# Channel sums of x² taken on TensorE block by block, and the additions of x left to VectorE alone, at the ends of the layers of a two-layer encoder

## The chip, the cores and the metric

The kernel runs on one core of one Trainium2 chip. The metric is the device time of one execution in microseconds (us). Engines are named as the profile names them: PE is TensorE's matmul, PEld its weight load, DVE is VectorE, ACT is ScalarE, POOL is GpSimd, SP is SyncE, which starts the weight transfers.

## The reference

Two layers of a streaming encoder over 256 prompt frames and 64 sample frames (320 tokens, width 1024). Layer 0 is a Mamba-2 mixer, layer 1 an attention with a shared latent; each is followed by a convolutional feed-forward. Every sub-layer is wrapped in norms:

```
def rmsnorm(x, g):
    xf = x.astype(F32)
    y = xf * lax.rsqrt(jnp.mean(xf * xf, axis=-1, keepdims=True) + EPS)
    return (y * g.astype(F32)).astype(x.dtype)
...
for layer in range(DEPTH):
    h = rmsnorm(x, norm_mix_pre[layer])
    mix = ...                                   # mixer of this layer
    x = x + rmsnorm(mix, norm_mix_post[layer])
    f, fbuf = conv_ffn(rmsnorm(x, norm_ffn_pre[layer]), ...)
    x = x + rmsnorm(f, norm_ffn_post[layer])
```

So at the end of a sub-layer y is normalized and added to x, and the next sub-layer needs the mean of the new x² over the 1024 channels of each token.

## The kernel before, in words

**Layout.** Channels lie on the 128 partitions. `x` is a tile of 8 blocks of 128 channels by 320 tokens, and so are `y` (the sub-layer's output) and `xgh`, `xgl`. Matmuls run at float32 quality in three passes (`mm3`): each operand is split into a rounded high part and the low rest (`xgh`/`xgl` for x, `wh`/`wl` or, for units split ahead of time, `eh`/`el` for weights), and high·high, high·low and low·high are summed. A weight unit is fetched by SP into `wr`, split by ACT (high, L327 or L330) and DVE (low, L329 or L331), and taken from a stream by `nextw`.

**The ends.** There are four places where a sub-layer begins with fresh x, all in `enter`. At the start of the program (`boundary=False`) x is loaded. The other three are ends of sub-layers: mixer to feed-forward in layer 0 (near 266 us), feed-forward to attention (near 510 us), attention to feed-forward in layer 1 (near 733 us). There `late_rstd` makes the scale 1/rms of y for each token on POOL (L340) and spreads it over the partitions by three transposes on PE (L359) into one PSUM tile; between these PE runs bfloat16 filler matmuls (L365). Then, for block k = 0..7, `enter` does

- DVE: y(k) times the scale, which is read from that PSUM tile (L442);
- x(k) plus y(k) (L446), on DVE for k = 0, 1, 2, 4, 6 and on POOL for k = 3, 5, 7;
- ACT: the high part xgh(k) (L411; block 0's is made by DVE, L444);
- DVE: the low part xgl(k-1) (L418, or L421 without a gain), and behind xgl(1) and xgl(2) the low part of a weight unit;
- ACT: the square of x(k-1) (L433, block 0's by L430), and POOL adds it to `xacc` (L434).

In this region DVE and ACT keep the written order (`manual_schedule`); all other order is chosen by the scheduler when the program is built. Every engine executes its own list strictly in order.

**What follows.** PE runs the first matmuls of the next sub-layer (`outer`): for each x block k, six output blocks of 128 columns, 18 matmuls of 320 columns (block 0 at L583, the others at L284 and L285; 12 matmuls at the program's start; at the attention nine at a time for blocks 4 to 7). Their output is scaled afterwards, so they don't wait for the mean of x². That comes from `toksum`: three float32 matmuls with `xacc` as weights and a column of ones (L352), which the profile shows as six weight loads and six matmuls; DVE turns the sums into a mean (L346), POOL into 1/rms (L340), PE spreads it.

**PSUM.** Eight banks are divided into pools: `pm` for outputs, `px` for scratch and `pr` for sums and spread scales. The attention has no `pr` (its pools are 5 `pm` and 3 `px`), so at its end the spread scale lies in a `px` tile; `ffn` closes these pools behind `enter` and opens 7 `pm` and 1 `pr`.

**Weights ahead.** `early_open` fetches and splits some units of the next sub-layer during the last matmuls of the mixer or the feed-forward; `EARLY` says how many at each of the three ends.

Of the kernel before, what the change touches and what calls it, by code (L numbers as in the profile page):

```python
# [11 lines left out]
AF = mybir.ActivationFunctionType  # L12
ALU = mybir.AluOpType
# [3 lines left out]
P = 128  # L17
T = 320
TP = 256
TS = 64  # L20
D = 1024
KD = 8
NBF = 22
EPS = 1e-6
# [15 lines left out]
AHEAD = 1, 2  # L40

RING = 2, 3, 2
EARLY = 1, 9, 3
HIGH = 2, 0, 2
PSA = dict(m=5, x=3)
PSF = dict(m=7, r=1)
# [8 lines left out]
TOK = 0, 128, 192  # L55
# [31 lines left out]
class Kern:  # L87
# [252 lines left out]
        self.nw_end = self.nc.gpsimd.tensor_tensor(out=r, in0=v, in1=self.half[:, 0:v.shape[1]], op=ALU.pow).ins  # L340
        return r

    def mean(self, src, dim, pool):

        v = self.t(pool, [P, 3], "nwv", bufs=3)
        self.nc.vector.tensor_scalar(v, src, 1.0 / dim, EPS, op0=ALU.mult, op1=ALU.add)  # L346
        return v

# [5 lines left out]

    def spread(self, r, ps=None):

        ps = self.pr() if ps is None else ps
        for c, l0 in enumerate(TOK):
            self.pe_end = self.nc.tensor.transpose(ps[:, l0:l0 + 128], r[:, c:c + 1].to_broadcast([P, P]), self.ident).ins  # L359
        return ps[:, :T]  # L360
# [35 lines left out]
            self.high_ahead(HIGH[b])  # L396
        return ps

    def enter(self, xgp, sp, tag, g=None, boundary=True):


        nc = self.nc
        tt, act = nc.vector.tensor_tensor, nc.scalar.activation
        r = self.late_rstd() if boundary else None
        xh = self.t(xgp, [P, KD, T], "xgh", F32R, bufs=1)
        xl = self.t(xgp, [P, KD, T], "xgl", F32R, bufs=1)
        acc = self.t(sp, [P, T], "xacc", bufs=1)
        self.xhigh = []

        def high(k):  # L410
            i = act(out=xh[:, k, :], in_=self.x[:, k, :], func=AF.Copy, scale=self.v(g, k) if g and k else 1.0)  # L411
            if boundary:
                self.xhigh.append(i.ins)

        def low(k):
            h = xh[:, k, :].bitcast(F32)
            if g and k:
                i = nc.vector.scalar_tensor_tensor(out=xl[:, k, :], in0=self.x[:, k, :], scalar=self.v(g, k), in1=h,  # L418
                                                   op0=ALU.mult, op1=ALU.subtract)
            else:  # L420
                i = tt(out=xl[:, k, :], in0=self.x[:, k, :], in1=h, op=ALU.subtract)  # L421
            self.low_end = i.ins
            if boundary and k in AHEAD:
                self.gate = i.ins
                if self.lows:
                    self.lows.pop(0)()

        def square(k):
            if k == 0:
                act(out=acc, in_=self.x[:, k, :], func=AF.Square)  # L430
                return
            s = self.t(sp, [P, T], tag, bufs=2)
            act(out=s, in_=self.x[:, k, :], func=AF.Square)  # L433
            nc.gpsimd.tensor_tensor(out=acc, in0=acc, in1=s, op=ALU.add)  # L434

        with self.region if boundary else ExitStack():
            for k in range(KD + 1):
                if k < KD:
                    xk = self.x[:, k, :]
                    if boundary:  # L440
                        yk = self.y[:, k, :]
                        tt(out=yk, in0=yk, in1=r, op=ALU.mult)  # L442
                        if k == 0:
                            tt(out=xh[:, k, :], in0=xk, in1=yk, op=ALU.add)  # L444
                        e = nc.gpsimd if k in (3, 5, 7) else nc.vector
                        e.tensor_tensor(out=xk, in0=xk, in1=yk, op=ALU.add)  # L446
                        if k:
                            high(k)
                        else:
                            low(k)  # L450
                    else:
                        high(k)
                        low(k)
                if boundary and k > 1:
                    low(k - 1)
                if k:
                    square(k - 1)
        if boundary:
            self.ends.pop(0)
        return xh, xl, acc  # L460

    def normalized(self, xgp, sp, g, rstd):

# [123 lines left out]
            s = slice(b * 128, b * 128 + 128)  # L587
            self.mm3(ps[b][:, :T], w[k][0][:, s], w[k][1][:, s], xh[:, k, :], xl[:, k, :], k == 0, k == KD - 1, behind)

    def outer(self, nblk, xh, xl, xacc, pool):  # L590

        ps = [self.pm() for _ in range(nblk)]
        a, b = OUT
        self.outer_part(ps, range(a), xh, xl)
        r = self.rstd_of(xacc, D, pool)
        self.gate = self.nw_end
        self.outer_part(ps, range(a, b), xh, xl, self.pe_end)
        r = self.rstd_sb(r, pool, "xr")
        self.outer_part(ps, range(b, KD), xh, xl, self.pe_end)
        self.xhigh = []  # L600
        return ps, r
# [96 lines left out]
    def ssm(self):  # L698
        nc, a = self.nc, self.a
        self.silus, self.exps, self.burst = [], [], []  # L700
        self.yg, self.dc, self.ea = {}, {}, {}
        with ExitStack() as st:
# [5 lines left out]
            with ExitStack() as s2:  # L708
                sx = ExitStack()
                xgp = self.pool(sx, "xn0", "right")  # L710
                sp = self.pool(s2, "ssm")
                self.ssave = self.t(sp, [P, 24, 2, 3], "ssave")
                with ExitStack() as s3:
# [7 lines left out]
                    nc.sync.dma_start(out=self.con, in_=a["con"][:, 0:CON["cos"][0]])  # L721
                    nc.sync.dma_start(out=self.vec[:, 8:], in_=a["vec"][:, 8:])
                    self.qd = KD
                    xh, xl, xacc = self.enter(xtp, dp, "xsq", "mix_pre0", False)
                    ps, rstd = self.outer(4, xh, xl, xacc, dp)
                    self.bt, self.ct, self.xs = {}, {}, {}
                    dt2 = self.ssm_dt(ps[0], rstd, sp, dp)
                    for i in range(1, 4):
# [306 lines left out]
    def ffn(self, i):  # L1035
        nc, a = self.nc, self.a
        with ExitStack() as st:
# [3 lines left out]
            with ExitStack() as s2:  # L1041
                xgp = self.pool(s2, f"xgf{i}")
                sp = self.pool(s2, f"fs{i}")
                fsave = self.t(sp, [P, 44, 2, 2], "fsave")
                xh, xl, xacc = self.enter(xgp, sp, "xsq", f"ffn_pre{i}")
                self.yst.close()
                self.psum(**(PSF, PSL)[i])
                ps, rstd = self.outer(6, xh, xl, xacc, sp)
                self.est.close()
                self.table(AF.Gelu_apprx_tanh)  # L1050
                xnh, xnl, steps = self.normalized(xgp, sp, f"ffn_pre{i}", rstd)
# [39 lines left out]
    def mla(self):  # L1091
        nc, a = self.nc, self.a
        tt, ts, stt = nc.vector.tensor_tensor, nc.vector.tensor_scalar, nc.vector.scalar_tensor_tensor
        with ExitStack() as st:
# [10 lines left out]
            with ExitStack() as s2:  # L1105
# [3 lines left out]
                oldt = self.t(sp, [P, 2, 256], "oldt")  # L1109
                nc.sync.dma_start(out=old, in_=a["old"].rearrange("p (a b) -> p a b", a=3))  # L1110
                nc.sync.dma_start(out=oldt, in_=a["oldt"].rearrange("p (a b) -> p a b", a=2))
                xh, xl, xacc = self.enter(xgp, sp, "xsq")
                self.yst.close()
                self.psum(**PSF)
                u = self.t(kp, [P, 2, T], "u")
# [5 lines left out]
                kv, ps = pk[:3], pk[3:]  # L1121
                self.outer_part(pk, range(4), xh, xl)
                self.outer_part(kv, range(4, 8), xh, xl)
                s = self.t(sp, [P, T], "xsq", bufs=2)
                nc.scalar.activation(out=kacc, in_=kv[0][:, :T], func=AF.Square)
                nc.scalar.activation(out=s, in_=kv[1][:, :T], func=AF.Square)
                tt(out=kacc, in0=kacc, in1=s, op=ALU.add)
# [6 lines left out]


                pt = self.pr()
                self.toksum(xacc, pt)
                self.toksum(kacc, pt, 3)
                vs = self.t(sp, [P, 6], "vs")
                ex = self.t(sp, [P, 3], "ex")  # L1140
                ts(vs[:, 0:3], pt[:, 0:3], 1.0 / D, EPS, op0=ALU.mult, op1=ALU.add)
                ts(ex, vs[:, 0:3], EPS, None, op0=ALU.mult)
                stt(out=vs[:, 3:6], in0=pt[:, 3:6], scalar=1.0 / 256, in1=ex, op0=ALU.mult, op1=ALU.add)
                self.outer_part(ps, range(5, 7), xh, xl, self.pe_end)
# [17 lines left out]
                for b in range(3):  # L1162
                    nc.scalar.activation(out=cqh[:, b, 0:TS], in_=cqh[:, b, T:].bitcast(F32), func=AF.Copy)
                    self.pgate = nc.gpsimd.tensor_copy(out=cql[:, b, 0:TS], in_=cql[:, b, T:].bitcast(F32)).ins
                    if b == 0:
                        nc.scalar.activation(out=qacc, in_=ps[b][:, :T], func=AF.Square)
                    else:
                        s = self.t(sp, [P, T], "xsq", bufs=2)
                        nc.scalar.activation(out=s, in_=ps[b][:, :T], func=AF.Square)
                        tt(out=qacc, in0=qacc, in1=s, op=ALU.add)  # L1170
                for dst, src in ((slice(0, 256), slice(0, 256)), (slice(512, 576), slice(256, 320))):
# [386 lines left out]
```

## Time and profile before

| | before |
|---|---|
| runs | 985.29, 985.29, 986.44 us (median 985.29) |
| the profiled execution | 985.59 us, span 983.8 us |
| PE busy | 960.0 us, 98% of the span |
| DVE, ACT, POOL busy | 738.8, 614.0, 353.5 us |

The profile is a record of one execution: which instruction ran on which engine when, and what it waited for. A line number is that of the kernel printed above. "PEclk" is the clock that PE was granted, as a share of full speed. A view by stretches gives each engine's busy time and number of instructions in that stretch. Times in a timeline are start and duration in us from the beginning of the span. Successive matmuls overlap, so the work of PE is read from the distance between their starts.

### The profile page before, as it was taken

To read this page: it belongs to the slowest core of one execution; us is meant where nothing else is said; L and a number is where in the kernel's file an instruction comes from. 1 tells how busy PE (TensorE), PEld (TensorE's weight loads), DVE (VectorE), ACT (ScalarE), POOL (GpSimd) and SP (SyncE) were. 2 spreads that over 40 slices of the span, in tenths; PEclk is the share of its full clock that TensorE was granted. 3 is DMA by queue.
4 is the path that set the end of the run, shared out by engine and by line. 5 is a ranking of instruction groups with operands and counts; after the bars stand their busy time and mean duration, and the time that the engine had idled before them with its cause. 6 is when DMAs were issued, how large, how long until landed. Compare 5 with 4: busy or idle time off the path is not lost.

```text
span 983.8 us, 17990 instructions
## 1 busy us (share of the span) xinstructions
PE 960.0 (98%) x6602; PEld 932.7 (95%) x6602; DVE 738.8 (75%) x1348; ACT 614.0 (62%) x1247; POOL 353.5 (36%) x560
## 2 busy tenths in 40 slices
PE   8799999999999999999999999999999999999997
PEld 8799999989989999999999899999999999999996
DVE  7989889975579998765547898885638999775432
ACT  7568988644556787654444677764645678665331
POOL 5822411000056875420017766520005777441000
PEclk9899999999999999999999999999999999999999
DMA  7465646443334545455631222233534454445541
GB/s 256 143 196 181 202 134 204 139 134 118 103 119 131 171 150 172 150 181 165 195 112 37 81 73 76 57 97 108 172 107 127 129 174 151 151 145 147 153 118 54
DMA packets 45945, 135.58 MB, mean 138 GB/s; under 512 B 5408, under 2 KB 10144, under 8 KB 45856
## 3 DMA queue, kind: packets, MB, share of 16 engines
q1 hardware_dynamic: 45712, 134.42, 43.9%
q8 instruction: 52, 0.85, 0.4%
q14 instruction: 37, 0.30, 0.1%
q10 hardware_dynamic: 144, 0.00, 0.0%
HBM read 130.29 MB, written 4.11 MB: 137 GB/s over the span
## 4 chain that ended last, share of the span: by engine, by line
PE 83%; DVE 9%; POOL 3%; ACT 2%; issue 2%; DMA 0%; SPq 0%; POOLq 0%; DVEq 0%; ACTq 0%
PE pm L284 47%; PE pm L285 23%; PE px L284 3%; PE px L285 1%; PE px L987 1%; PE px L970 1%; PE pr L352 1%; POOL xacc L434 1%; DVE wl L329 1%; PE px L978 1%; ACT wh L327 1%; POOL xn L470 1%; DVE xnl L331 1%; DVE cv L670 1%; PE px L953 1%
## 5 line engine op out<-in xcount | busy, mean ns | idle before, releaser
L329 DVE TENSOR_TENSOR wl<-wr,wh 128x1024 fp32r<-128x1024 f32 (+2 forms) x204 | 242.9, 1191 | 108.7 <-ACT wh L327 107.6
L327 ACT ACTIVATE wh<-wr 128x1024 fp32r<-128x1024 f32 (+4 forms) x235 | 227.7, 971 | 149.1 <-PE pm L284 131.5
L284 PE MATMUL pm<-xnh,wh 128*128 128x320 f32 x768 | 239.2, 312 | 0.2 <-DVE ext L660 0.2
L284 PE MATMUL pm<-xnl,wh 128*128 128x320 f32 x768 | 239.3, 312 | 0.0
L285 PE MATMUL pm<-xnh,wl 128*128 128x320 f32 x768 | 238.2, 310 | 0.0
L284 PEld LDWEIGHTS pm<-xnl,wh 128*128 128x128 f32 x768 | 144.2, 188 | 3.0 <-issue 3.0
L285 PEld LDWEIGHTS pm<-xnh,wl 128*128 128x128 f32 x768 | 144.2, 188 | 1.7 <-issue 1.7
L284 PEld LDWEIGHTS pm<-xnh,wh 128*128 128x128 f32 x768 | 144.2, 188 | 1.5 <-issue 0.7
L285 PE MATMUL pm<-ah,wl 128*128 128x320 f32 x424 | 131.3, 310 | 0.0
L284 PE MATMUL pm<-al,wh 128*128 128x320 f32 x424 | 131.2, 310 | 0.0
L284 PE MATMUL pm<-ah,wh 128*128 128x320 f32 x424 | 131.1, 310 | 0.0
L670 DVE SCALAR_TENSOR_TENSOR cv<-ext,vec,cv 128x322 f32<-128x322 f32 x176 | 98.2, 569 | 6.1 <-ACT cv L668 3.6
L664 POOL COPY fsave<-ext 128x2 f32<-128x2 f32 x88 | 71.1, 808 | 50.5 <-ACT ext L658 46.9
L340 POOL TENSOR_TENSOR rk<-nwl,half 128x3 f32<-128x3 f32 x4 | 3.4, 851 | 216.5 <-DVE nwl L391 216.5
L284 PEld LDWEIGHTS pm<-ah,wh 128*128 128x128 f32 x424 | 79.5, 188 | 1.0 <-issue 1.0
L285 PEld LDWEIGHTS pm<-ah,wl 128*128 128x128 f32 x424 | 79.6, 188 | 0.2 <-issue 0.2
L284 PEld LDWEIGHTS pm<-al,wh 128*128 128x128 f32 x424 | 79.6, 188 | 0.0
L284 PE MATMUL pm<-xgh,wh 128*128 128x320 f32 x236 | 68.6, 320 | 7.2 <-ACT xs L689 5.9
L285 PE MATMUL pm<-xgh,wl 128*128 128x320 f32 x236 | 74.2, 317 | 0.7 <-DVE wl L331 0.7
L284 PE MATMUL pm<-xgl,wh 128*128 128x320 f32 x236 | 74.1, 317 | 0.5 <-DVE xgl L418 0.5
L668 ACT ACTIVATE cv<-ext,vec 128x322 f32<-128x322 f32 x88 | 57.0, 653 | 15.1 <-POOL ext L655 9.7
L329 POOL TENSOR_TENSOR wl<-wr,wh 128x512 fp32r<-128x512 f32 (+2 forms) x31 | 43.7, 1424 | 25.2 <-ACT wh L327 22.7
(384 smaller groups left out, 2196.5 us busy)
## 6 DMA issues: line engine op xcount, KB each, us to landing
wr<-w_up SPq DMA_DIRECT2D x76, 512.0 KB, 3.3
wr<-w_in SPq DMA_DIRECT2D x37, 512.0 KB, 3.9
wr<-w_dn SPq DMA_DIRECT2D x32, 512.0 KB, 3.6
wr<-w_out SPq DMA_DIRECT2D x16, 512.0 KB, 3.4
wr<-w_o SPq DMA_DIRECT2D x16, 512.0 KB, 3.3
wr<-w_up_k SPq DMA_DIRECT2D x16, 384.0 KB, 3.4
wr<-w_dn SPq DMA_DIRECT2D x16, 384.0 KB, 3.2
dc<-acd SPq DMA_DIRECT2D x8, 512.0 KB, 6.0
```

Source lines behind the costliest of these rows:

```text
L284: for i in (mm(out, wh, xh, start=first, stop=False), mm(out, wh, xl, start=False, stop=False), mm(out, wl, xh, start=False, stop=last)):
L285: mm(out, wl, xh, start=False, stop=last)):
L327: self.high_ins = nc.scalar.activation(out=hdst, in_=src, func=AF.Copy).ins
L329: return lambda: e.tensor_tensor(out=ldst, in0=src, in1=hdst.bitcast(F32), op=ALU.subtract)
L331: return lambda: nc.vector.scalar_tensor_tensor(out=ldst, in0=src, scalar=scale, in1=hdst.bitcast(F32), op0=ALU.mult, op1=ALU.subtract)
L352: i = self.nc.tensor.matmul(ps[:, o + b:o + b + 1], acc[:, l0:l0 + 128], self.ones[:, 0:1], start=True, stop=True)
L434: nc.gpsimd.tensor_tensor(out=acc, in0=acc, in1=s, op=ALU.add)
L470: nc.gpsimd.tensor_tensor(out=xn, in0=self.x[:, k, :], in1=rstd, op=ALU.mult)
L664: nc.gpsimd.tensor_copy(out=rows_out[:, 0, :], in_=ext[:, TP:TP + m])
L668: nc.scalar.activation(out=c, in_=ext[:, 0:n], func=AF.Identity, scale=w(0), bias=b)
L670: nc.vector.scalar_tensor_tensor(out=c, in0=ext[:, i:i + n], scalar=w(i), in1=c, op0=ALU.mult, op1=ALU.add)
L953: nc.tensor.transpose(xt_[:n, j * 128:j * 128 + 128], xs[j][:, l0:l0 + n], self.ident)
```

## The change

The squares of x are no longer added up by POOL. Each block's square goes from ACT straight to PE: three matmuls with the square as weights and a column of ones, accumulated over the eight blocks in three columns of PSUM (L432 in the changed kernel). At the three ends of sub-layers these are columns 320 to 322 of the very PSUM tile that holds the spread scale of y; at the start it is a tile of their own. `enter` returns the mean instead of `xacc`, `toksum(xacc)` is gone. The three additions x(k) plus y(k) that POOL did are on DVE, so POOL has nothing left in the loop of `enter`. `EARLY` is 2 instead of 1 at the first end: one more unit of `w_up` is fetched and split during the mixer's last matmuls.

```diff
-EARLY = 1, 9, 3
+EARLY = 2, 9, 3
...
     def spread(self, r, ps=None):
-        ps = self.pr() if ps is None else ps
+        ps = self.spread_tile = self.pr() if ps is None else ps
...
-    def enter(self, xgp, sp, tag, g=None, boundary=True):
+    def enter(self, xgp, sp, tag, g=None, boundary=True, mean=None):
...
-        acc = self.t(sp, [P, T], "xacc", bufs=1)
+        sums = self.spread_tile if boundary else self.pr()
...
         def square(k):
-            if k == 0:
-                act(out=acc, in_=self.x[:, k, :], func=AF.Square)
-                return
-            s = self.t(sp, [P, T], tag, bufs=2)
+            s = self.t(sp, [P, T], tag, bufs=3)
             act(out=s, in_=self.x[:, k, :], func=AF.Square)
-            nc.gpsimd.tensor_tensor(out=acc, in0=acc, in1=s, op=ALU.add)
+            for b, l0 in enumerate(TOK):
+                nc.tensor.matmul(sums[:, T + b:T + b + 1], s[:, l0:l0 + 128], self.ones[:, 0:1], start=k == b == 0, stop=k == KD - 1 and b == 2)
...
-                        e = nc.gpsimd if k in (3, 5, 7) else nc.vector
-                        e.tensor_tensor(out=xk, in0=xk, in1=yk, op=ALU.add)
+                        tt(out=xk, in0=xk, in1=yk, op=ALU.add)
...
-        return xh, xl, acc
+        return xh, xl, self.mean(sums[:, T:T + 3], D, sp, mean)
...
-    def outer(self, nblk, xh, xl, xacc, pool):
+    def outer(self, nblk, xh, xl, xv, pool):
...
-        r = self.rstd_of(xacc, D, pool)
+        r = self.newton(xv, pool, "rk")
...
-                self.toksum(xacc, pt)
                 self.toksum(kacc, pt, 3)
```

The diff leaves open where the scheduler puts the new matmuls in PE's list, and what waits the shared tile brings. This is read from the built programs, at three places. Numbers behind a name are those of the tile; x blocks are not told apart.

PE at the third end (attention to feed-forward), before: the spread scale, filler matmuls, then the first matmuls of `outer`.

```order
L359 MATMUL px_9100<-con_71,rk_9098 128x128 x3
...
L365 MATMUL pm_9082<-warm_75 128x256
L583 MATMUL pm_9191<-xgh_9122,wh_8963 128x320
L583 MATMUL pm_9192<-xgh_9122,wh_8963 128x320
...
L284 MATMUL pm_9191<-xgh_9122,wh_8998 128x320
```

The same place now.

```order
L359 MATMUL px_9141<-con_71,rk_9139 128x128 x3
...
L365 MATMUL pm_9123<-warm_75 128x256
L432 MATMUL px_9141<-ones_73,xsq_9172 128x1 x3
L432 MATMUL px_9141<-ones_73,xsq_9182 128x1 x3
L432 MATMUL px_9141<-ones_73,xsq_9192 128x1 x3
...
L432 MATMUL px_9141<-ones_73,xsq_9234 128x1 x3
L580 MATMUL pm_9251<-xgh_9163,wh_9004 128x320
L580 MATMUL pm_9252<-xgh_9163,wh_9004 128x320
```

All eight squares stand ahead of the first matmul of `outer`.

DVE at the same place, with the semaphores that each row waits for, before:

```order
L442 TENSOR_TENSOR y_8708<-y_8708,px_9100 128x320
L446 TENSOR_TENSOR x_72<-x_72,y_8708 128x320 [waits DVE_49]
L442 TENSOR_TENSOR y_8708<-y_8708,px_9100 128x320
L446 TENSOR_TENSOR x_72<-x_72,y_8708 128x320 [waits DVE_49]
L418 SCALAR_TENSOR_TENSOR xgl_9123<-x_72,vec_70,xgh_9122 128x320 [waits Activation_49]
L329 TENSOR_TENSOR wl_9115<-wr_8961,wh_9114 128x768 [waits DMAHW1_49]
```

and now (blocks 1, 2 and the beginning of 3):

```order
L440 TENSOR_TENSOR y_8749<-y_8749,px_9141 128x320
L443 TENSOR_TENSOR x_72<-x_72,y_8749 128x320 [waits DVE_49]
L440 TENSOR_TENSOR y_8749<-y_8749,px_9141 128x320 [waits PE_49]
L443 TENSOR_TENSOR x_72<-x_72,y_8749 128x320 [waits DVE_49]
L418 SCALAR_TENSOR_TENSOR xgl_9164<-x_72,vec_70,xgh_9163 128x320 [waits Activation_49]
L329 TENSOR_TENSOR wl_9156<-wr_9002,wh_9155 128x768 [waits DMAHW1_49]
L440 TENSOR_TENSOR y_8749<-y_8749,px_9141 128x320 [waits PE_49]
```

From block 2 on, y(k) waits for PE. By the counts of the semaphore, what it waits for is the square of block k-2; and that square waits for y(k-1) on DVE, since both use the same tile. It is so at all three ends.

PE at the first end (mixer to feed-forward), where before all 18 matmuls of a block stand together; now:

```order
L284 MATMUL pm_3315<-xgh_3221,wh_3091 128x320
L432 MATMUL pr_3199<-ones_73,xsq_3230 128x1 [waits DVE_49,Activation_49]
L432 MATMUL pr_3199<-ones_73,xsq_3230 128x1 x2
L284 MATMUL pm_3310<-xgl_3222,wh_3091 128x320 [waits DVE_49]
L285 MATMUL pm_3310<-xgh_3221,wl_3092 128x320
```

The square of block k-1 stands behind the first six matmuls of block k (those with xgh alone), and the other twelve, which need xgl(k), stand behind the square. At the second end it is the same for blocks 1 to 4, and with three and six matmuls from block 5 on. At the program's start all eight squares stand within blocks 0 to 3.

More of the change, by code (lines that the diff above doesn't have):

```diff
@@ L341, in newton, with mean @@
         return r
-    def mean(self, src, dim, pool):
-        v = self.t(pool, [P, 3], "nwv", bufs=3)
+    def mean(self, src, dim, pool, v=None):
+        v = self.t(pool, [P, 3], "nwv", bufs=3) if v is None else v
         self.nc.vector.tensor_scalar(v, src, 1.0 / dim, EPS, op0=ALU.mult, op1=ALU.add)
@@ L723, in ssm @@
                     self.qd = KD
-                    xh, xl, xacc = self.enter(xtp, dp, "xsq", "mix_pre0", False)
-                    ps, rstd = self.outer(4, xh, xl, xacc, dp)
+                    xh, xl, xv = self.enter(xtp, dp, "xsq", "mix_pre0", False)
+                    ps, rstd = self.outer(4, xh, xl, xv, dp)
                     self.bt, self.ct, self.xs = {}, {}, {}
@@ L1044, in ffn @@
                 fsave = self.t(sp, [P, 44, 2, 2], "fsave")
-                xh, xl, xacc = self.enter(xgp, sp, "xsq", f"ffn_pre{i}")
+                xh, xl, xv = self.enter(xgp, sp, "xsq", f"ffn_pre{i}")
                 self.yst.close()
                 self.psum(**(PSF, PSL)[i])
-                ps, rstd = self.outer(6, xh, xl, xacc, sp)
+                ps, rstd = self.outer(6, xh, xl, xv, sp)
                 self.est.close()
@@ L1111, in mla @@
                 nc.sync.dma_start(out=oldt, in_=a["oldt"].rearrange("p (a b) -> p a b", a=2))
-                xh, xl, xacc = self.enter(xgp, sp, "xsq")
+                vs = self.t(sp, [P, 6], "vs")
+                xh, xl, _ = self.enter(xgp, sp, "xsq", mean=vs[:, 0:3])
                 self.yst.close()
@@ L1123, in mla @@
                 self.outer_part(kv, range(4, 8), xh, xl)
-                s = self.t(sp, [P, T], "xsq", bufs=2)
+                s = self.t(sp, [P, T], "xsq", bufs=3)
                 nc.scalar.activation(out=kacc, in_=kv[0][:, :T], func=AF.Square)
@@ L1136, in mla @@
                 pt = self.pr()
-                self.toksum(xacc, pt)
                 self.toksum(kacc, pt, 3)
-                vs = self.t(sp, [P, 6], "vs")
                 ex = self.t(sp, [P, 3], "ex")
-                ts(vs[:, 0:3], pt[:, 0:3], 1.0 / D, EPS, op0=ALU.mult, op1=ALU.add)
                 ts(ex, vs[:, 0:3], EPS, None, op0=ALU.mult)
@@ L1167, in mla @@
                     else:
-                        s = self.t(sp, [P, T], "xsq", bufs=2)
+                        s = self.t(sp, [P, T], "xsq", bufs=3)
                         nc.scalar.activation(out=s, in_=ps[b][:, :T], func=AF.Square)
```

## The prediction

> **What bounds the kernel now.** I read the page first, its busy times and its chain:
>
> ```profile
> span 983.8 us, 17990 instructions
> ...
> PE 960.0 (98%) x6602; PEld 932.7 (95%) x6602; DVE 738.8 (75%) x1348; ACT 614.0 (62%) x1247; POOL 353.5 (36%) x560
> ...
> PE 83%; DVE 9%; POOL 3%; ACT 2%; issue 2%; DMA 0%; SPq 0%; POOLq 0%; DVEq 0%; ACTq 0%
> ```
>
> PE carries 83% of the chain that ended last and is idle for 983.8 - 960.0 = 23.8 us in all. Time that the change adds to PE, or in which PE must wait, has almost no slack to go into. So the question is how busy PE was where the change acts. The view by stretches, for the three ends of sub-layers and then for some stretches of 3.41 us that I need for the clock:
>
> ```profile
> core 0: us, PE busy (x) PEld busy (x) DVE busy (x) ACT busy (x) POOL busy (x), PEclk, DMA share, GB/s
> 270.00:287.00 17.00, 15.91 (x108) 15.58 (x107) 16.28 (x25) 8.85 (x18) 10.00 (x9) 1.00 0.34 108
> 514.00:531.00 17.00, 16.89 (x116) 16.62 (x114) 14.51 (x24) 8.53 (x20) 13.44 (x12) 1.00 0.12 35
> 736.00:750.00 14.00, 13.68 (x91) 13.21 (x91) 12.48 (x21) 5.73 (x13) 7.64 (x8) 1.00 0.24 77
> ...
> 284.92:288.33 3.41, 1.54 (x9) 1.02 (x7) 2.83 (x5) 3.16 (x7) 2.28 (x3) 1.00 0.45 154
> 288.33:291.74 3.41, 3.33 (x12) 3.09 (x13) 1.03 (x2) 1.11 (x2) 1.63 (x1) 0.50 0.68 186
> ...
> 39.16:42.57 3.41, 0.00 (x0) 0.00 (x0) 3.41 (x6) 2.85 (x4) 3.37 (x4) 1.00 0.39 147
> 42.57:45.98 3.41, 2.23 (x8) 2.26 (x9) 3.41 (x8) 3.23 (x7) 2.50 (x5) 0.50 0.51 159
> 650.14:653.55 3.41, 2.27 (x14) 1.77 (x13) 3.19 (x12) 3.41 (x13) 0.00 (x0) 1.00 0.18 72
> 653.55:656.96 3.41, 3.41 (x30) 3.40 (x30) 3.20 (x10) 2.74 (x8) 0.00 (x0) 1.00 0.02 5
> ```
>
> At the second and third end PE is busy 16.89 of 17 and 13.68 of 14 us: the POOL work that the change removes there is hidden already. Only the first end and the program's start show waits, in the list of PE's waits:
>
> ```profile
> PE pr L352 <- POOL xacc L434: 0.9, 1, 0.9
> ...
> PE pm L284 <- ACT wh L330: 1.3, 1, 1.3
> PE pm L285 <- DVE wl L331: 0.7, 1, 0.7
> ```
>
> **The change part by part.**
>
> *POOL's work.* By lines:
>
> ```profile
> L434 POOL TENSOR_TENSOR xacc<-xacc,xsq 128x320 f32<-128x320 f32 x28 | 29.6, 1056 | 24.8 <-ACT xsq L433 24.2
> L446 POOL TENSOR_TENSOR x<-x,y 128x320 f32<-128x320 f32 x9 | 10.5, 1162 | 7.5 <-DVE y L442 7.5
> ```
>
> Those 40.1 us leave POOL, and none of it was on PE's path but the waits above. The nine additions cost DVE nine times 0.49 us (timeline below); they lie inside the cycles that I work out next.
>
> *The squares on PE.* What three such matmuls cost in a running stream is seen where `toksum` stood in one:
>
> ```profile
> 752.58 0.31 PE L285 MATMUL pm<-xgh,wl 128*128 128x320 f32 x1
> 752.73 0.76 PE L352 MATMUL pr<-ones,xacc 128*128 128x1 f32 x6
> 753.35 0.39 PE L284 MATMUL pm<-xgh,wh 128*128 128x320 f32 x1
> 753.58 0.31 PE L284 MATMUL pm<-xgl,wh 128*128 128x320 f32 x1
> ```
>
> Matmuls of 320 columns start 0.147 us apart (0.15 here), so the one at 753.58 would have started at 752.88: 0.70 us. Eight squares for one `toksum` are 7 x 0.70 = 4.9 us of PE at each end.
>
> *The new waits.* y(k) now waits for the square of block k-2. The steps of that cycle, all from the third end:
>
> ```profile
> 731.71 0.44 ACT L485 ACTIVATE ysq<-pm 128x320 f32<-128x320 f32 x1 [6.26 <-PE pm L285]
> 732.20 0.83 PE L352 MATMUL px<-ones,ysq 128*128 128x1 f32 x6 [0.53 <-ACT ysq L485]
> 733.07 0.16 DVE L391 SCALAR_TENSOR_TENSOR nwl<-px,nwv 128x3 f32<-128x3 f32 x1 [3.06 <-PE px L352]
> 736.01 1.14 PE L583 MATMUL pm<-xgh,wh 128*128 128x320 f32 x6
> 736.93 0.48 DVE L442 TENSOR_TENSOR y<-y,px 128x320 f32<-128x320 f32 x1
> 737.45 0.49 DVE L446 TENSOR_TENSOR x<-x,y 128x320 f32<-128x320 f32 x1
> 737.97 0.56 ACT L411 ACTIVATE xgh<-x,vec 128x320 fp32r<-128x320 f32 x1 [2.42 <-DVE x L446]
> 738.37 0.49 DVE L446 TENSOR_TENSOR x<-x,y 128x320 f32<-128x320 f32 x1
> 738.44 0.46 ACT L430 ACTIVATE xacc<-x 128x320 f32<-128x320 f32 x1
> 738.78 0.55 DVE L418 SCALAR_TENSOR_TENSOR xgl<-x,vec,xgh 128x320 fp32r<-128x320 f32 x1
> 739.38 0.41 PE L284 MATMUL pm<-xgl,wh 128*128 128x320 f32 x1 [0.31 <-DVE xgl L418]
> ```
>
> From the start of a square on PE to the DVE instruction that waits for it: 733.07 - 732.20 = 0.87 us. From y(k) to x(k): 0.52. From x(k) to xgl(k-1): 0.41. From xgl to PE: 0.60. From x(k) to xgh(k): 0.52; from there to the square of block k-1 on ACT, which stands behind it: 0.47; from a square on ACT to PE: 0.49.
>
> *First and second end.* PE's list is: six matmuls of block k, square k-1, twelve matmuls of block k with xgl(k). That xgl(k) stands on DVE behind y(k+1), which waits for square k-1. So after each square PE stands still until 0.87 + 0.52 + 0.41 + 0.60 = 2.40 us from the square's start, less the 0.70 that the square itself takes: 1.70 us. This happens for y(2) to y(7), six times: 10.2 us. Nothing hides it, as PE's list holds nothing else there. ACT isn't late for it: the next square is ready 0.52 + 0.47 + 0.49 us after x(k), while PE still has 15 to 18 matmuls (2.2 to 2.6 us) to run. Bounds per wait: 0.48 less if xgl's DVE time counts as overlapped, 0.5 more if a weight split (0.95 us and more on DVE) gets in between.
>
> Squares and waits make 10.2 + 4.9 = 15.1 us at each of the two. At the first end the waits of 1.3 and 0.7 us go, since fetches and splits get 15 us more, and with them the stretch at PEclk 0.50: its 12 matmuls ran 0.12 us slower each, 1.4 us. So -3.4 us there.
>
> *Third end.* All squares stand ahead of `outer`, and PE has nothing to do beside them. The first square starts at 738.44 + 0.49 = 738.93. Each next one follows after 0.87 + 0.52 + 0.52 + 0.47 + 0.49 = 2.87 us, so the seventh starts at 738.93 + 6 x 2.87 = 756.15; the eighth is right behind it, and `outer` begins at 756.15 + 2 x 0.70 = 757.55 instead of 736.01: 21.5 us later, with all its work still to do (13.68 us of it was done by 750 before). The old `toksum`'s 0.70 goes: 20.8 us. Bounds: 17 us if DVE and ACT steps overlap by 0.6 us a cycle, 24 if weight splits hold up y(k).
>
> *The clock.* The rows of 3.41 us show how PE's clock follows its work: a stretch with nine matmuls of 320 columns, or none, is followed by one at 0.50; one with 14 by full speed. At 0.50 those matmuls start 0.267 us apart:
>
> ```profile
> 288.85 0.47 PE L284 MATMUL pm<-xgh,wh 128*128 128x320 f32 x1
> 289.12 0.47 PE L284 MATMUL pm<-xgl,wh 128*128 128x320 f32 x1
> ```
>
> In the new cycle of the first end, 18 matmuls (2.65 us) and 2.40 us with none of that size, a stretch of 3.41 us holds ten or fewer in about 0.38 of its positions. Of nine such stretches in 30 us that makes three at half speed. A stretch has PE at work for two thirds; at half speed it loses 0.45 of that, 1.0 us. So +3 us at the first end, +4 at the second, whose last cycles hold nine matmuls only. At the third, no matmul of 320 columns runs for 21 us: from the second or third square on the clock should be at 0.50. A square's price there is shown nowhere; I take 0.70 x 0.267/0.147 = 1.27, as for the matmuls, between unchanged (0.70) and that: six squares by 0.57 make 3.4 us, and `outer` starts with one to one and a half slow stretches, 1.9 us. So +5.3. Bounds for all three: 0, if squares count as work for the clock, and +37, if both loops run at half speed (six times 2.7 us each) and the third loses 5.3.
>
> The Trainium skill (TensorE: Matmul & The Clock Gate, What's actually happening) says that the clock is halved after at least one idle window of about 3.4 us. By that rule none of the new gaps (1.70 us, and 2.2 us at the third end) would halve it, and the sum would lack its 12.3 us: 1033. The trace disagrees: 284.92:288.33 was not idle, with PE busy 1.54 of 3.41 us, and the next stretch ran at 0.50.
>
> *The rest.* At the start squares wait for nobody's y, but stand within blocks 0 to 3, so block 4 waits for the last one:
>
> ```profile
> 15.34 0.46 ACT L433 ACTIVATE xsq<-x 128x320 f32<-128x320 f32 x1
> ...
> 21.45 0.54 PE L359 MATMUL pr<-con,rk 128*128 128x128 f32 x3
> ```
>
> 15.34 + 0.49 + 0.70 = 16.53, then three blocks of 12 matmuls (5.3 us) and the spread at 21.8 instead of 21.45: +0.4, between -2 (DVE, rid of POOL beside it, splits weights sooner) and +2. `EARLY` = 2 moves one fetch on SP's queue and one split of ACT and DVE ahead into the mixer's last matmuls; I count nothing, since PE waited for neither there. If it did, it would cost one split, 1 us. The scheduler also shuffles other rows; 0 +- 2.
>
> *Sum.* First end 15.1 - 3.4 + 3 = 14.7; second 15.1 + 4 = 19.1; third 20.8 + 5.3 = 26.1; start 0.4: +60.3 us. On the profiled execution's 985.6 this is 1045.9; that execution stands 0.3 us above the runs' median of 985.29, so 1046 rounded.
>
> **The rivals.**
>
> *The clock stays full*: the waits as above without 12.3 us, 1033. For it speaks that the squares keep PE's weight loads going; against it the row with 1.54 us busy.
>
> *Half speed throughout the loops*: each square halves the next stretch, and slow cycles hold fewer matmuls. 12.3 becomes 37: 1070. Against it: a slow stretch with 12 matmuls was followed by full speed (288.33:291.74).
>
> *The waits are not there at the first two ends*, because PE reaches a square late and DVE is through by then. Then 4.9 us of PE each and the third end remain: 985.6 + 4.9 - 3.4 + 4.9 + 26.1 = 1018. Against it: xgl stands behind the waiting y in DVE's list.
>
> *Faster*: DVE, which shared these stretches with POOL, is quicker alone, and PE was waiting for DVE. This needs y(k) never to be held by a square. It could win the 3.4 us of the first end, the 0.9 at the start and the idle 1.1 + 0.1 + 0.3 us of the three stretches, so 980; it decides only if the six waits at an end cost nothing and the third end's squares are no barrier. The order of the lists excludes it almost.
>
> **How the numbers follow.** 55% for the forecast (1035 to 1056 by itself), 20% for the full clock, 10% for half speed, 11% for the waits missing at two ends, 3% for faster; 1% for no change. The range from 1027 to 1062 takes in the first two and some of half speed, and leaves out 1018 and below. Slower by over 0.2%, about what this kernel's runs can tell from no change, is 96%; faster 3%; within 1%.
>
> **What would show it.** Right: at the third end the first matmul of `outer` some 21 us or more after the spread, with eight groups of squares about 2.9 to 3.6 us apart ahead of it; at the other two, after each square a wait of PE for xgl of about 1.7 us, six times; y's rows waiting for PE; more stretches with PEclk at 0.50. Wrong: `outer` at the third end beginning within 2 us of the spread, or no wait of y for PE. Half the error, if there is one, should lie in the clock.

## The result: 1067 us, slower, and 21 us later than forecast

| | median of runs (lowest to highest) | profiled execution |
|---|---|---|
| before | 985.29 us (983.77 to 986.44, 6 runs) | 985.6 us, span 983.8 |
| after | 1067.39 us (1062.27 to 1080.75, 6 runs) | 1077.46 us, span 1075.6 |

The ratio is 1.0847, with a 95% interval from 1.0813 to 1.0882. The page of the changed kernel:

```profile
span 1075.6 us, 18305 instructions
...
PE 1017.6 (95%) x6770; PEld 988.5 (92%) x6770; DVE 730.2 (68%) x1357; ACT 614.6 (57%) x1247; POOL 302.8 (28%) x523
```

POOL lost 50.7 us of work; the prediction had counted the 40.1 us of its additions. PE took on 57.6 us of busy time and 34.2 us of idle time. The idle time is in the list of PE's waits (first number the sum, then how often, then the longest):

```profile
PE px L432 <- ACT xsq L430: 15.3, 7, 2.9
PE pm L284 <- DVE xgl L418: 9.4, 6, 1.6
PE pm L284 <- DVE xgl L421: 9.0, 6, 1.5
```

These are the three waits of the prediction: the third end's squares (L432), and six waits for xgl at the first end (L418) and at the second (L421), 1.5 to 1.6 us each.

This execution lies 10 us above the median, so stages are better read from a second profile of the same kernel, `after_again` below, at 1066.21 us. `toksum` over yacc stands at the beginning of each end; its four rows mark the stages. The timeline of before:

```profile
264.13 0.72 PE L352 MATMUL pr<-ones,yacc 128*128 128x1 f32 x6
505.25 0.72 PE L352 MATMUL pr<-ones,yacc 128*128 128x1 f32 x6
729.09 0.72 PE L352 MATMUL px<-ones,yacc 128*128 128x1 f32 x6
967.59 0.72 PE L352 MATMUL pr<-ones,yacc 128*128 128x1 f32 x6
```

and of after_again:

```profile
267.71 0.72 PE L352 MATMUL pr<-ones,yacc 128*128 128x1 f32 x6
529.02 0.72 PE L352 MATMUL pr<-ones,yacc 128*128 128x1 f32 x6
782.70 0.72 PE L352 MATMUL px<-ones,yacc 128*128 128x1 f32 x6
1047.90 0.72 PE L352 MATMUL pr<-ones,yacc 128*128 128x1 f32 x6
```

| from mark to mark | before | after_again | difference | forecast |
|---|---|---|---|---|
| start and state-space part | 264.13 | 267.71 | +3.6 | +0.4 |
| first end and feed-forward | 241.12 | 261.31 | +20.2 | +14.7 |
| second end and attention | 223.84 | 253.68 | +29.8 | +19.1 |
| third end and feed-forward | 238.50 | 265.20 | +26.7 | +26.1 |

Of the 20 us that the forecast is short, 16 lie at the first two ends. The second end takes longer in this profile than elsewhere: 250.5 us in the first profile (+26.6), and 250.5 to 251.4 in four others in which this stage is unaltered.

### The profile page after: what moved, and what is told of

It reads as the page before. It is cut to its first block, busy times and chain, and to the rows that moved or that the text cites. A ratio compares the mean times of both kernels' runs of the same rounds, so it can differ in the third digit from the quotient of the medians.

```text
span 1075.6 us, 18305 instructions
## 1 busy us (share of the span) xinstructions
PE 1017.6 (95%) x6770; PEld 988.5 (92%) x6770; DVE 730.2 (68%) x1357; ACT 614.6 (57%) x1247; POOL 302.8 (28%) x523
## 4 chain that ended last, share of the span: by engine, by line
PE 83%; DVE 10%; ACT 3%; DMA 2%; issue 2%; SPq 0%; ACTq 0%; DVEq 0%
PE pm L284 46%; PE pm L285 22%; PE px L284 3%; PE pr L432 2%; PE px L285 1%; PE pm L580 1%; PE px L432 1%; PE px L967 1%; DMA dc<-acd 1%; DVE y L440 1%; DVE x L443 1%; PE px L984 1%; DVE wl L329 1%; ACT wh L327 1%; PE px L975 1%
## 5 line engine op out<-in xcount | busy, mean ns | idle before, releaser
L329 DVE TENSOR_TENSOR wl<-wr,wh 128x1024 fp32r<-128x1024 f32 (+3 forms) x203 | 239.2, 1179 | 122.8 <-ACT wh L327 122.2
L284 PE MATMUL pm<-xgh,wh 128*128 128x320 f32 x230 | 72.8, 346 | 3.1 <-DVE ext L657 2.1
```

The lines of the kernel that those rows point to most:

```text
L284: for i in (mm(out, wh, xh, start=first, stop=False), mm(out, wh, xl, start=False, stop=False), mm(out, wl, xh, start=False, stop=last)):
L329: return lambda: e.tensor_tensor(out=ldst, in0=src, in1=hdst.bitcast(F32), op=ALU.subtract)
```

## One end read closely

The squares at the first end of after_again, six matmuls to a row (two for each of three token blocks):

```profile
276.94 0.72 PE L432 MATMUL pr<-ones,xsq 128*128 128x1 f32 x6
281.98 0.72 PE L432 MATMUL pr<-ones,xsq 128*128 128x1 f32 x6
288.55 0.72 PE L432 MATMUL pr<-ones,xsq 128*128 128x1 f32 x6
295.12 0.72 PE L432 MATMUL pr<-ones,xsq 128*128 128x1 f32 x6
301.60 0.82 PE L432 MATMUL pr<-ones,xsq 128*128 128x1 f32 x6
307.97 1.04 PE L432 MATMUL pr<-ones,xsq 128*128 128x1 f32 x6
312.75 2.55 PE L432 MATMUL pr<-ones,xsq 128*128 128x1 f32 x12
```

The first cycle is 281.98 - 276.94 = 5.04 us; the prediction's 18 matmuls (2.65) and 2.40 us make 5.05. The steps inside it, on DVE and then on PE:

```profile
282.74 0.49 DVE L440 TENSOR_TENSOR y<-y,pr 128x320 f32<-128x320 f32 x1 [2.69 <-PE pr L432]
283.26 0.49 DVE L443 TENSOR_TENSOR x<-x,y 128x320 f32<-128x320 f32 x1
283.67 0.54 DVE L418 SCALAR_TENSOR_TENSOR xgl<-x,vec,xgh 128x320 fp32r<-128x320 f32 x1
284.27 0.41 PE L284 MATMUL pm<-xgl,eh 128*128 128x320 f32 x1 [1.57 <-DVE xgl L418]
```

y stood still 2.69 us for the square on PE, and PE then 1.57 us for xgl. So the waits are as forecast. But the next cycles are 6.57, 6.57, 6.48 and 6.37 us, with the same 18 matmuls. The same time by stretches of the clock:

```profile
core 0: us, PE busy (x) PEld busy (x) DVE busy (x) ACT busy (x) POOL busy (x), PEclk, DMA share, GB/s
281.31:284.72 3.41, 1.84 (x15) 1.76 (x14) 1.95 (x4) 0.92 (x2) 0.00 (x0) 1.00 0.28 100
284.72:288.14 3.42, 3.42 (x15) 3.42 (x14) 0.36 (x1) 0.00 (x0) 0.00 (x0) 0.50 0.45 153
288.14:291.55 3.41, 1.84 (x15) 1.76 (x15) 1.44 (x3) 0.92 (x2) 0.00 (x0) 1.00 0.00 0
291.55:294.96 3.41, 3.41 (x15) 3.41 (x14) 0.00 (x0) 0.00 (x0) 0.00 (x0) 0.50 0.00 0
```

PE's wait falls into a stretch at full speed, and the next one runs at 0.50; that one holds only matmuls and brings the clock back, just in time for the next wait. At half speed the cycle becomes 6.57 us, nearly two stretches (6.83), so that each wait meets a fast stretch again and halves the one after it. The prediction had spread the waits evenly over the positions of a stretch and got three slow ones in 30 us; in this profile the two take up step. The step is not always the same: the first profile's cycles at this end are 5.03, 6.11, 7.81, 6.36 and 6.38 us, the long one with three slow stretches in a row.

At the third end the squares stand ahead of `outer`, with the wait for ACT's next square in brackets:

```profile
788.03 0.49 PE L359 MATMUL px<-con,rk 128*128 128x128 f32 x3
792.56 0.83 PE L432 MATMUL px<-ones,xsq 128*128 128x1 f32 x6 [2.94 <-ACT xsq L430]
...
809.44 1.44 PE L432 MATMUL px<-ones,xsq 128*128 128x1 f32 x6 [2.06 <-ACT xsq L430]
812.94 2.72 PE L432 MATMUL px<-ones,xsq 128*128 128x1 f32 x12 [2.06 <-ACT xsq L430]
815.53 1.95 PE L580 MATMUL pm<-xgh,wh 128*128 128x320 f32 x6
```

The period there is 3.50 us (809.44 to 812.94), where 2.87 + 0.57 = 3.44 was forecast (a square at half speed was taken as 1.27 us, and lasts that long in the rows of the second end below), and `outer` begins 27.5 us after the spread instead of 1.6.

## The experiments

**The kernel once more.** Same file.

> The changed kernel once more, unaltered. In its profiled run PE's clock stayed at half until 33.11 us and the first spread came at 35.66 us; in second_own_tile and third_interleaved, which have the same instructions at the start, the clock was up at 4.8 us and the spread came at 22.7 and 22.6. Theory (the late clock belongs to that one execution, because half speed with one-column squares among the matmuls keeps itself up once it is met): this profile has the spread at 22 to 23 us and a time of 1062 to 1068, the ends as before at +20, +26, +26. Rival (the late clock belongs to the kernel): the spread at 35 us again, and about 1077.

Measured: 1066.39 us median (1063.08 to 1078.03, 4 runs). The spread is at 22.64 us, so the late start belongs to the first profile's execution. In that one PE ran like this at the start:

```profile
19.46:22.87 3.41, 3.41 (x17) 3.41 (x15) 1.40 (x3) 1.50 (x4) 0.00 (x0) 1.00 0.02 5
...
29.70:33.11 3.41, 3.41 (x14) 3.41 (x14) 0.87 (x2) 1.24 (x2) 0.00 (x0) 1.00 0.00 0
33.11:36.52 3.41, 3.41 (x26) 3.40 (x25) 2.21 (x4) 2.05 (x4) 0.00 (x0) 1.00 0.48 150
```

The column of the clock says 1.00 in all of them, but the trace has no record of the clock before its first change, at 33.11; the counts tell (17 and 14 matmuls in a stretch, then 26), as do the distances: matmuls of 320 columns start 0.267 us apart up to there. PE had no gap in these stretches and still stayed at half speed while squares were among its matmuls; the first stretch without any (29.70) released it. The Trainium skill (TensorE: Matmul & The Clock Gate, What's actually happening) has the gate open after one busy window of about 3.4 us. Here seven such windows in a row, from 5.80 to 29.70 us, busy from end to end, did not open it.

The same start has more than these two courses. In second_filled (below) the clock came up at 10.07 us and the spread at 25.04. In first_filled it was up at 4.04 us and fell again, behind a stretch in which PE was busy from end to end with three groups of squares among ten matmuls of 320 columns:

```profile
14.28:17.69 3.41, 3.41 (x30) 3.41 (x29) 1.22 (x5) 1.28 (x4) 1.10 (x3) 1.00 0.90 360
17.69:21.10 3.41, 3.41 (x15) 3.41 (x15) 0.89 (x2) 0.84 (x2) 1.25 (x1) 0.50 0.02 7
```

**The start, other ways.** start_wide sums into 128 equal columns at the start; start_on_gpsimd has GpSimd there again.

```diff
-nc.tensor.matmul(sums[:, T + b:T + b + 1], s[:, l0:l0 + 128], self.ones[:, 0:1], ...)
+n, o = (1, T + b) if boundary else (128, 128 * b)
+nc.tensor.matmul(sums[:, o:o + n], s[:, l0:l0 + 128], self.ones[:, 0:n], ...)
...
```

> The changed kernel, but at the program's start alone the squares' sums are made with 128 equal columns (ones of 128 columns, one of them read) instead of one column; all other instructions and their order stay. Theory (matmuls of one column do not count as work for PE's clock, so that the eight groups at the start hold it at half speed until 33 us): with 128 columns the clock comes up at about 8 to 12 us, the first spread is at 22 to 25 us instead of 35.66, and the time falls by 11 to 14 us, to about 1055. Rival (the clock stays low for another reason, such as late weights or the order of the blocks, and the groups cost their own time only): the clock comes up at 33 us as now, and the time stays within 3 us or rises, since there is more to stream.

> The changed kernel, but at the program's start alone the squares are summed on GpSimd and reduced by toksum, as in the kernel before. Theory (the prediction's 0.4 us for the start is the term that failed; the start and the stage behind it took 17.3 us): the spread is back at 21.5 us, and the time falls by 14 to 18 us, to 1050 to 1053. Rival (the start costs only what PE spends on seven more groups, 7 x 0.70 = 4.9 us, and the rest is made up later): -3 to -6 us.

Measured: start_wide 1062.95 us (1062.75 to 1065.15, 4 runs), spread at 22.6; start_on_gpsimd 1060.19 us (1056.28 to 1061.98, 4 runs), spread at 21.5. Both expectations rested on the late clock of the first profile, and both missed. Against after_again, wide sums are 3.4 us ahead between medians, but not by the start: their first mark is at 267.68 us (267.71 in after_again), and the difference is in the second end, which is unaltered (250.50 against 253.68). The start with GpSimd is 6 to 7 us ahead; its first mark comes 3.5 us earlier.

The same two on the kernel before, with nothing else of the change (`if not boundary:` in `square`, sums in `self.pr()`, no `toksum` there):

> The kernel before with the start's squares alone summed on TensorE with one column, as in the changed kernel. In after_again the spread at the start came 1.2 us later than before and the stage behind it ended 3.6 us later; in the first profile of the changed kernel the clock was late and both were 14 to 17 us later. Theory (the place has two courses, decided by where the clock's stretches fall): most runs at 987 to 990, about one in four at 999 to 1003. Rival 1 (the late clock has nothing to do with the start's squares): all runs at 987 to 990. Rival 2 (the prediction's 0.4 us): all within 1 us of 985.3.

> As before_start_pe, but with 128 equal columns in each of the start's sums instead of one. Theory (what keeps the clock at half is that a matmul of one column does not count as work): no run at 999 or above, all at 986 to 990. Rival (it is the time that the groups take, not their columns): the same spread of times as before_start_pe, or all of them 1 to 3 us later for the longer sums.

Measured: before_start_pe 992.71 us (988.50 to 1003.44; ratio 1.0089, 1.0058 to 1.0120); its seven runs are 988.5 to 995.8 and two at 1000.1 and 1003.4. before_start_wide 989.71 us (987.54 to 991.68, 6 runs; ratio 1.0052, 1.0034 to 1.0070). So the start by itself costs 7.5 us with one column and 4.5 with 128, between medians, not 0.4. The high times came with one column only: 10 of the 37 runs of kernels with one-column sums at the start were 11.6 to 18.5 us above the lowest of their kernel, none of the 18 with wide sums or GpSimd there. Only one such execution was profiled, so that a late clock explains the other nine is likely, not shown.

**A tile of its own at the second end.**

```diff
-PSF = dict(m=7, r=1)
+PSF = dict(m=6, r=2)
-sums = self.spread_tile if boundary else self.pr()
+sums = self.spread_tile if boundary and 3 - len(self.ends) not in (1,) else self.pr()
```

> The changed kernel, but at the second end the squares are summed in a PSUM tile of their own instead of the spread's (the PSUM pool of that stage and of the first feed-forward becomes 6 + 2 banks instead of 7 + 1). Theory (y(k) waits for a square only because of the shared tile; these waits and the clock that they pull down make the second end's 26.7 us): no wait of y for PE there, PE's six waits for xgl (9.0 us) are gone, fewer stretches at half speed, and the second end costs 5 to 10 us instead of 26.7; the time falls by 16 to 22 us. Rival 1 (the waits go, but the squares themselves keep pulling the clock down): -9 us. Rival 2 (the waits are hidden work of DVE and come back under another name): within 3 us of the changed kernel.

Measured: 1045.05 us (1042.48 to 1056.98, 4 runs; ratio 1.0640, 1.0577 to 1.0703), 21 below the changed kernel. The row `xgl L421` is gone from PE's waits. In the view by stretches of its second end PE does not stop, and the clock stays up:

```profile
541.00:547.00 6.00, 6.00 (x46) 6.00 (x46) 5.83 (x15) 4.24 (x10) 0.00 (x0) 1.00 0.02 6
```

From mark to mark this stage takes 228.6 us: +4.8 against before, where the squares alone were put at 7 x 0.70 = 4.9. Waits and clock together cost the rest of the 29.8 (of 26.6 in the first profile), and both come from the shared tile.

**The waits kept, the clock held up.** After each of squares 1 to 6 twelve matmuls on zeros, in a spare bank (`PSF = dict(m=6, r=2)` as in second_own_tile).

```diff
+fill = self.pr() if boundary and len(self.ends) == 2 else None
...
+if fill is not None and 0 < k < 7:
+    self.pe_end = i.ins
+    self.busy(fill, 12)
```

> The changed kernel with the shared tile and all its waits kept, but at the second end twelve matmuls on zeros (256 columns, as the kernel has them elsewhere to keep PE busy) behind each of the squares 1 to 6, into a spare PSUM bank (that stage's pool and that of the first feed-forward are 6 + 2 banks as in second_own_tile). They add 1.5 us of PE to each wait of about 1.5 us. Theory (the term that failed is the clock: the waits themselves are as forecast, and half speed adds 10 to 13 us to an end): with PE kept at work the cycles there are 5.0 us instead of 5.4 to 6.5, and the second end costs 14 to 17 us instead of 26.6; the time falls by 9 to 12 us against the changed kernel. Rival (the cycles are long for another reason, such as weight splits on DVE ahead of y): no gain, or up to 6 us slower where the fillers stand in the way.

Measured: 1061.89 us (1059.62 to 1074.52, 4 runs). The squares of the second end, in after_again:

```profile
540.78 0.72 PE L432 MATMUL pr<-ones,xsq 128*128 128x1 f32 x6
547.09 0.95 PE L432 MATMUL pr<-ones,xsq 128*128 128x1 f32 x6
553.37 1.27 PE L432 MATMUL pr<-ones,xsq 128*128 128x1 f32 x6
...
577.25 1.27 PE L432 MATMUL pr<-ones,xsq 128*128 128x1 f32 x6
580.13 1.27 PE L432 MATMUL pr<-ones,xsq 128*128 128x1 f32 x6
```

and with the fillers:

```profile
544.41 0.72 PE L433 MATMUL pr<-ones,xsq 128*128 128x1 f32 x6
549.38 0.72 PE L433 MATMUL pr<-ones,xsq 128*128 128x1 f32 x6
549.97 1.47 PE L365 MATMUL pr<-warm 128*128 128x256 bf16 x12
...
571.20 0.72 PE L433 MATMUL pr<-ones,xsq 128*128 128x1 f32 x6
573.09 0.73 PE L433 MATMUL pr<-ones,xsq 128*128 128x1 f32 x6
```

Without fillers the last cycles went wholly at half speed, as the view by stretches of after_again has it:

```profile
566.50:571.90 5.40, 3.89 (x16) 3.81 (x16) 1.39 (x3) 0.83 (x2) 0.00 (x0) 0.50 0.00 0
571.90:577.00 5.10, 3.59 (x16) 3.51 (x16) 3.62 (x6) 2.74 (x6) 1.06 (x2) 0.50 0.00 0
```

With fillers, cycles of 6.3 us become 4.97. From the first square to the seventh, with 87 matmuls of 320 columns between them either way, it is 26.8 us instead of 36.5 (33.4 to 36.5 in the seven profiles with this loop unaltered): work that computes nothing makes this part of the loop 6.6 to 9.7 us shorter. The whole stage takes 245.6 us, 8.1 less than in after_again and 4.8 to 5.7 less than in the five other profiles. That is less than the loop's own gain, since just behind the loop PE now waits 2.2 us for kacc and falls to half speed there. The total falls by 4.5 us between medians; in this profile the part up to the first mark was 1.9 us longer than in after_again and the first end 1.7.

The same at the first end (spare banks taken from the stage before, whose mark comes 15 us later by it):

> As second_filled, but at the first end: the shared tile and its waits kept, twelve matmuls on zeros behind each of the squares 1 to 6, into a spare bank (pools there 4+2+2 and 6+2 banks, which cost the stage before it some 14 us in all_own_tiles; only the first end is read here). Theory (half speed makes the cycles of 6.57 us out of 5.04): all five cycles of 18 matmuls at 4.9 to 5.1 us, from the second to the seventh square 24.2 to 26 us instead of 30.77, and no stretch at half speed among them. Rival (the long cycles are weight splits ahead of y on DVE): cycles of 6 us and more remain, with PE busy on zeros.

Measured: 1068.87 us (1066.57 to 1071.85, 4 runs). Its first cycle, ahead of the first filler, is slow; then:

```profile
298.41 0.72 PE L433 MATMUL pr<-ones,xsq 128*128 128x1 f32 x6
303.44 0.72 PE L433 MATMUL pr<-ones,xsq 128*128 128x1 f32 x6
308.48 0.72 PE L433 MATMUL pr<-ones,xsq 128*128 128x1 f32 x6
313.51 0.72 PE L433 MATMUL pr<-ones,xsq 128*128 128x1 f32 x6
```

Cycles of 5.03 to 5.04 us, and no stretch at half speed among them, where after_again has 6.57, 6.57 and 6.48: some 1.5 us less for each. From the second square to the seventh it is 22.0 us instead of 30.8, but that is not all clock, since with these pools 18 fewer matmuls of 320 columns stand between the two squares. The first end as a whole costs +14.3 instead of +20.2.

**The third end interleaved.** `PSA = dict(m=5, x=2, r=1)`: attention gives up a `px` bank for a `pr`, and the third end gets the order of the first.

> The changed kernel, but attention's PSUM pool has 5 + 2 + 1 banks instead of 5 + 3, so that the spread's tile at the third end lies in the bank that stays the same pool afterwards, and outer's matmuls no longer stand behind all eight squares: by the built program the third end then has the first end's order, six matmuls, a square, twelve matmuls. Theory (the third end costs 26.1 as forecast because outer waits for the last square): its cost becomes that of the first end, 15 to 21 us instead of 26.7, and the time falls by 5 to 11 us. Rival (with half the clock either way, interleaving brings nothing, or attention loses by the missing bank what the end gains): within 3 us.

Measured: 1075.37 us (1065.75 to 1082.52, 4 runs, two of them among the ten high ones). Both parts of the rival are in the marks: the third end is 1.8 us shorter (263.4 against 265.2), and attention 5.2 us longer (199.3 against 194.1 from its spread to the next mark). With its 18 matmuls between two squares the cycle is 6.3 us and more; interleaving bought little, since waits and half speed stayed.

**Own tiles everywhere**, and the start on GpSimd.

> The changed kernel with the squares of all three ends in PSUM tiles of their own (pools 4+2+2, 6+2, 4+2+2, 6+2 banks in the order of the program) and with the start's squares on GpSimd as before. Theory (beyond the waits and their clock, the squares cost PE 7 x 0.70 = 4.9 us an end, and the first end still gains its 3.4): 985 + 3 x 4.9 - 3.4 = 996, between 992 and 1003. Rival 1 (the sums as such, in short matmuls between the long ones, pull the clock down too): each end 10 us or more, 1012 and above. Rival 2 (the ends are as in the theory, but the stages with fewer banks lose, as attention lost 8 us in third_interleaved): 1000 to 1015, with the loss in those stages.

Measured: 1023.39 us (1021.65 to 1024.62, 4 runs; ratio 1.0389, 1.0371 to 1.0408). Rival 2, and larger than expected. From mark to mark the first end costs +0.4 and the third +4.4; the second loop costs +4.9 up to the spreads behind it. But the state-space part loses 14.2 us and attention 14.3 us by the banks that were taken from them.

**The other two parts of the change, on the kernel before.** EARLY = 2, 9, 3 and all additions of x on VectorE, together and apart.

> The kernel before with the two other parts of the change alone: all additions of x on VectorE and one more weight unit split ahead; the squares stay on GpSimd. Theory (PE's waits of 1.3 and 0.7 us at the first end and the stretch at half speed behind them are what can be won): 1 to 3.4 us faster, 982 to 984. Rival (both are hidden, or the addition on VectorE delays y and xgl by as much): within 1 us of 985. Rival 2 (three more additions on VectorE, 0.49 us each, hold up the chain at each end): 1 to 3 us slower.

> The kernel before with one more weight unit split ahead (EARLY = 2, 9, 3) and nothing else of the change. before_adds_early was 3.2 us faster than before, and its first end 3.7 us shorter. Theory (the 3.7 us are PE's waits for a weight split at the first end, 1.3 + 0.7 us, and the slow stretch behind them, so the split that is made ahead wins them): all of it here, 981.5 to 983. Rival (the additions of x on VectorE win it, by ending the waits for GpSimd at the first end): 985 here, and 982 in before_adds.

> The kernel before with all additions of x on VectorE and nothing else of the change. Theory (the split ahead alone makes the gain): within 1 us of 985.25, the three additions being beside PE's work. Rival (the additions make the gain): 982 to 983.

| | median | runs | ratio, 95% interval |
|---|---|---|---|
| before_adds_early | 982.04 | 10 | 0.9968, 0.9958 to 0.9978 |
| before_early | 981.42 | 12 | 0.9971, 0.9958 to 0.9983 |
| before_adds | 984.53 | 12 | 0.9995, 0.9984 to 1.0006 |

The additions do nothing that can be measured, and the split ahead is worth 3 to 4 us: in before_early PE's waits of 1.3 and 0.7 us at the first end are gone, and that stage is 3.0 us shorter. before_early is faster than both kernels of this study.

**The split ahead within the change**, EARLY = 1, 9, 3 in the changed kernel:

> The changed kernel with the weight units split ahead as before (EARLY = 1, 9, 3). Theory (in the changed kernel PE's waits of 1.3 and 0.7 us at the first end are gone in any case, since its loop is 15 us and more longer, so that the split made ahead wins nothing): within 2 us of the changed kernel, 1063 to 1068. Rival (the split ahead is worth its 3 to 4 us here too): 1068 to 1071, with PE's waits for a weight split at the first end.

Measured: 1069.25 us (1065.99 to 1077.90, 4 runs; ratio 1.0889, 1.0836 to 1.0942), 2 to 3 us above the changed kernel and inside its spread. No wait for a weight split is in its list; its first end is 2.4 us longer, with one more long cycle (6.20 us instead of 4.78 for the sixth). It stays unclear.

## Where the prediction was right, and where it failed

- **Direction and mechanism were right.** y(k) waits for square k-2, PE for xgl(k), and the third end's squares stand ahead of `outer`. The waits were put at 1.70 us and are 1.5 to 1.6; the squares at 4.9 us an end and are 4.8 where they stand alone (second_own_tile).
- **The third end was right:** +26.7 for +26.1, with a period of 3.50 us for 3.44.
- **The first end's -3.4 us** fits: the two waits for a weight split are gone from PE's lists in both profiles of the changed kernel and in after_early1, and where they go in the kernel before (before_early, before_adds_early) this stage is 3.0 and 3.7 us shorter.
- **The step that failed is the clock at the first and second end**, put at +3 and +4. Taking from each stage's growth the squares (4.9), the measured waits (9.4 and 9.1) and, at the first end, the -3.4, what is left for the clock is 9.3 us at the first end and 15.8 at the second (12.7 in the first profile); these are estimates. The fillers show part of it directly: 6.6 to 9.7 us of the second loop, and 1.5 us for each of three cycles at the first end. The prediction treated where a wait falls in a stretch as chance. But a slow stretch changes the cycle, and the lengthened cycle can keep in step with the stretches, as it does in after_again. At the second end, with nine matmuls between the last squares, the clock did not come back at all between 566.50 and 577.00 us. The rival "half speed throughout the loops" (1070) was nearest, given 10%, though the first loop went at half speed only every other stretch. The argument against it, that a slow stretch with 12 matmuls was followed by full speed, is true of single stretches (284.72:288.14 above) and says nothing of the next wait. The boundary that the prediction drew, between nine matmuls and fourteen, rested on an attention stretch whose fourteen are of 128 to 512 columns; it is not a sharp one, since behind full-speed stretches with ten matmuls of 320 columns the clock fell in one case (first_filled, 14.28:17.69) and stayed up in another (second_filled, 16.89:20.31).
- **The start was mis-sized too:** +0.4 with bounds from -2 to +2, against +3.6 in after_again (1.2 up to the spread, 2.4 behind it). In the profiled execution of the changed kernel it was +17.3, with a clock that came up at 33.11 us instead of 4.83. Bounds that hold no clock were too narrow for a place where PE's work changes while its clock is still low.
- **The rivals "full clock" (1033), "waits missing" (1018) and "faster" (980)** are refuted by the slow stretches, by the rows `xgl L418` and `L421`, and by the time.
- **EARLY at nothing** is wrong for the kernel before (-3.8 us between medians). Within the change it is unclear: the waits that it removes go there in any case, and are counted in the -3.4.

The sum, with after_again's terms in place of the forecast's, is 3.6 + 20.2 + 29.8 + 26.7 = 80.3 us on a span that grew by 80.6.

## What to carry to other kernels

Before moving a sum to TensorE, look at which tile it is put in: beside a tile that another engine still reads, the sum and its readers wait for each other block by block, and the order of the lists shows it before anything runs. Where PE has a repeating wait (here 1.5 us), price it as the wait and the slow clock behind it, and work the cycle out again at half speed before counting slow stretches; filling such waits with matmuls on zeros at one end brought 4.5 us of the whole time, and a tile of its own there brought 21. Taking a PSUM bank for it from a stage that needs it can give most of this back: at each of the first and the third end an own tile won 20 to 22 us, and the stage before lost 14.

## What was not expected of the hardware

- Half speed in a PE that never stops: up to 33 us at the start, while groups of one-column matmuls stood among those of 320 columns, and in first_filled for one stretch behind such groups. What such a group consists of is in the lines of L432 at the start, for that execution and then for after_again (least, median and most ns of one):

```profile
L432 PEld LDWEIGHTS pr<-ones,xsq x48: 330/333/333, 5.9 to 27.7; 128*128 128x128 f32 x48
L432 PE MATMUL pr<-ones,xsq x48: 205/352/353, 6.2 to 27.8; 128*128 128x1 f32 x48
```

```profile
L432 PEld LDWEIGHTS pr<-ones,xsq x48: 187/192/193, 5.4 to 17.1; 128*128 128x128 f32 x48
L432 PE MATMUL pr<-ones,xsq x48: 164/250/251, 5.6 to 17.2; 128*128 128x1 f32 x48
```

  Each matmul of one column has a weight load of 0.19 us beside it (0.33 at half speed): a group is nearly all weight loads. That streamed columns count for the clock, and loads do not, is suggested by the ten runs with 128 columns, none of them high, and not settled.
- A loop of 5.04 us that becomes 6.57 us, where waits and clock stretches of 3.41 us fall into step.
